# U products of 40 tokens from gathered rows: narrower U chunks, a longer build stage, three row buffers

## The chip, the cores and the metric

The kernel runs on one core of a Trainium2 chip. The metric is the device time of one execution in microseconds. It computes one decoder layer for 512 tokens of width 1024 in float32: a mixer (Mamba-2 heads and latent attention) and then a PEER channel mixer, which chooses among 16384 experts. The change lies in the second part.

## The reference, cut to what matters

```python
def peer(x, w_query, sub_keys, u_table, v_table):      # blocks of 128 tokens
    q = (xb @ w_query).reshape(T, 8, 2, 128)
    s = einsum('thkd,hknd->thkn', q, sub_keys)
    sv, si = top_k(s, 16)                               # each half of each head
    cand_s = sv[:, :, 0, :, None] + sv[:, :, 1, None, :]
    cand_i = si[:, :, 0, :, None] * 128 + si[:, :, 1, None, :]
    top_s, top_pos = top_k(cand_s, 16)
    expert_idx = take_along_axis(cand_i, top_pos)       # 8 x 16 = 128 experts a token
    gate = softmax(top_s)
    act = gelu(einsum('td,thkd->thk', xb, u_table[expert_idx]))
    return einsum('thk,thkd->td', gate * act, v_table[expert_idx])
```

Each token uses 128 of the 16384 experts: the gate times gelu(u_e . x), times the row v_e, summed. Layer norms follow with a residual.

## The kernel before, in words

The 512 tokens are treated in two ways. **Blocks 0 to 2** (384 tokens) are computed densely: for each of 128 *chunks* of 128 experts, TensorE forms u.x for all of the chunk's experts (a *U chunk*, `u_half` at L1295, two halves of 12 matmuls in three-pass float32r), ScalarE applies Gelu into an `act` tile, VectorE multiplies by the gate matrix G (`v_prep`, L1429; G is zero where a token does not use an expert), and TensorE accumulates G.act times v (a *V chunk*, `v_mm`, 18 matmuls of 512 columns). **Block 3** (128 tokens) is computed by gathering: GpSimd fetches the rows u_e and v_e by indirect DMA and VectorE forms dots and sums (`gather`, L1488).

The last UG = 32 tokens of block 2 are a mixture. Their U products come from gathered rows (`ug_fetch`, `ug_dots`, L1128 to L1145): the 32 x 128 pairs of token and expert are laid out as 128 partitions x 32 columns; for column n GpSimd gathers 128 rows of u into a `urow` buffer (UROWS = 4 of them), and VectorE multiplies a row by the token's input `UR["x"]` and sums it, which is one *dot* (L1137). Their products gate x gelu, scaled, then stand in G itself (`ug_head`, L1147, writes them into `gT`), and so U chunks need only NU = 384 - 32 = 352 columns; `v_prep` copies G's last 32 columns as they are (L1437).

The work around the change has this order, all written out by hand, since the kernel records it under a manual schedule:

- The index search for blocks 0 to 2 ends in `decode` (L1033), which yields the expert numbers and gates `IJG[b]`, calls `ug_index` for block 2, two dots, and `g_head(0)`.
- `build_g` (L1187) makes G in 48 *steps* of 8 tokens. `hot(n)` on VectorE writes a one-hot pair (`ij`, L1195) and its product with the gates (`g`, L1202). The product covers a high and a low float16 part; for steps in LOWA, the even ones from 2 to 42, VectorE makes the high part alone (half the size), and ScalarE the low part in 8 copies (L1227), placed behind the evictions of the step before. TensorE multiplies the parts (16 matmuls of 128 columns, L1221 and L1222), ScalarE evicts the result (L1224), and every fourth step G goes to DRAM.
- `g_head(b)` (L1170) transposes the next 16 steps' gates and indices on TensorE; ScalarE copies them, and VectorE subtracts for the low part (L1183).
- `drive` (L1350) fills TensorE with halves of U chunks. It compares two clocks of estimated time, `tm[0]` for TensorE (T_U = 3.9 a U chunk) and `tm[1]` for VectorE, and issues a half when the first is not ahead, or when a minimum (`least`) asks for it. U chunks may run ahead only as far as there is room: LEAD = 56 `act` tiles, of which KEEP = 42 exist from the start, and 14 in the room of the pool `ug` (rows and inputs of the dots), which opens when the dots are done.
- After `build_g` the remaining U chunks up to LEAD follow, then V chunks, alternating with U chunks until these are through, and the gather of block 3 goes on beside them, paced by `GS` and ENDU so that it ends some chunks before the last V chunk. The V items from 121 on (LASTC = 120) use freed tiles and are multiplied block by block at the end, followed by the last layer norms.

Weights come through one stream (`Stream`): SP's queue loads 512 KB into one of three raw buffers (L93), ScalarE makes the rounded high part (L111), VectorE the difference (a *split*, L121), three buffers of each.

Of the kernel before, what the change touches and what calls it, by code (L numbers as in the profile page):

```python
# [11 lines left out]
F32 = mybir.dt.float32  # L12
# [3 lines left out]
I32 = mybir.dt.int32  # L16
U32 = mybir.dt.uint32
AF = mybir.ActivationFunctionType
OP = mybir.AluOpType
# [5 lines left out]
D = 1024  # L25
# [3 lines left out]
NEG = -1.0e30  # L29
SCALE = 192.0 ** -0.5  # L30
NT = 384
UG = 32
NU = NT - UG
LEAD = 56
KEEP = 42
UROWS = 4
RES = 2
LASTC = 120
T_U = 3.9
T_Q = 6.3  # L40
ROWS = 5
ENDU = 12
WV = 0.86
GST = (1, 3, 5, 7)
LOWA = range(2, 44, 2)
# [10 lines left out]
def tile_block(ctx: ExitStack, tc: tile.TileContext, I, out):  # L56
    nc = tc.nc
    ctx.enter_context(tc.manual_schedule())
    V, A, T, G = nc.vector, nc.scalar, nc.tensor, nc.gpsimd
# [158 lines left out]
    xsp = dram.tile([NB, 128, D], F32, name="xsp")  # L218
# [3 lines left out]
    ugi = dram.tile([UG, 128], I32, name="ugi")  # L222
    ugg = dram.tile([UG, 128], F32, name="ugg")
# [375 lines left out]
    for i in range(13):  # L599
        ps = proj(i)  # L600
# [511 lines left out]

    GT, UR = {}, {}

    def ug_index(tmp):
        ijg = IJG[2]
        f = lambda z: z.rearrange("p h k -> p (h k)")
        ix = tmp[:, :128].bitcast(I32)
        V.scalar_tensor_tensor(ix, f(ijg[:, 0]), 128.0, f(ijg[:, 1]), op0=OP.mult, op1=OP.add)
        G.dma_start(ugi, ix[128 - UG:])  # L1120
        G.dma_start(ugg, f(ijg[128 - UG:, 2]))
        G.dma_start(UR["ix"], bass.AP(tensor=ugi.tensor, offset=ugi.offset, ap=[[UG, 128 // UG], [128, UG], [1, UG]]))
        G.dma_start(UR["g"], ugg)
        for n in range(UROWS):
            ug_fetch(n)
        UR["dots"] = ug_dots()

    def ug_fetch(n):  # L1128
        if n < UG:
            UR[n] = ug.tile([128, D], F32, name="urow", bufs=UROWS)  # L1130
            G.indirect_dma_start(out=UR[n], out_offset=None, in_=I["u"],
                                 in_offset=bass.IndirectOffsetOnAxis(ap=UR["ix"][:, n:n + 1], axis=0))

    def ug_dots():
        for n in range(UG):
            r = UR.pop(n)
            V.scalar_tensor_tensor(r, r, 1.0, UR["x"], op0=OP.mult, op1=OP.mult, accum_out=UR["hd"][:, n:n + 1])  # L1137
            ug_fetch(n + UROWS)
            yield 1.2
        A.activation(UR["hd"], UR["hd"], AF.Gelu)  # L1140
        G.dma_start(bass.AP(tensor=ugh.tensor, offset=ugh.offset, ap=[[UG, 128 // UG], [128, UG], [1, UG]]), UR["hd"])
        G.dma_start(UR["w"], ugh)
        close(ug)
        aps.append(pool("act2"))
        yield 0.1  # L1145
# [24 lines left out]
    def g_head(b):  # L1170
        ijg = IJG.pop(b)
        ps = px()
        for x, e in enumerate((0, 1, 0, 2)):
            T.transpose(ps[:, x * 128:(x + 1) * 128], ijg[:, e].rearrange("p h k -> p (h k)"), ident)
        ijT = ijp.tile([128, 8, 2, 2, 8], F16, name="ijT", bufs=2)
        gT = ijp.tile([128, 16, 2, 8], F16, name="gT", bufs=2)
        gL = ijp.tile([128, 16, 8], F32, name="gL", bufs=2)
        gv = ps[:, 384:512].rearrange("p (n t) -> p n t", t=8)
        for r in range(2):
            src = bass.AP(tensor=ps.tensor, offset=ps.offset + r * 136, ap=[ps.ap[0], [128, 2], [16, 8], [1, 8]])  # L1180
            A.activation(ijT[:, :, r].rearrange("p n e t -> p e n t"), src, AF.Copy)
        A.activation(gT[:, :, 0], gv, AF.Copy, scale=GSC)
        V.scalar_tensor_tensor(gT[:, :, 1], gv, GSC, gT[:, :, 0], op0=OP.mult, op1=OP.subtract)  # L1183
        A.activation(gL, gT[:, :, 1], AF.Copy)
        GT[b] = ijT, gT, gL

    def build_g():  # L1187
        jij = gb.tile([128, 4, 4, 128, 2], F16, name="ij")

        def hot(n):  # L1190
            ijT, gT, gL = GT[n // 16]
            r = n % 2
            col = ijT[:, n % 16 // 2, r].rearrange("p e (q c) -> p (e q) c", c=2)
            b2 = [128, 8, 128, 2]
            V.tensor_tensor(jij[:, 2 * r:2 * r + 2].rearrange("p e q i c -> p (e q) i c"), iotaE[:, None].to_broadcast(b2),  # L1195
                            col[:, :, None, :].to_broadcast(b2), op=OP.is_equal)
            oj, oi = jij[:, 1 + r], jij[:, 3 * r]
            g = gb.tile([128, 2, 4, 128, 2], F16, name="g", bufs=2)
            ne = 1 if n in LOWA else 2
            b4 = [128, ne, 4, 128, 2]  # L1200
            gv = gT[:, n % 16, :ne].rearrange("p e (q c) -> p e q c", c=2)
            V.tensor_tensor(g[:, :ne], oi[:, None].to_broadcast(b4), gv[:, :, :, None, :].to_broadcast(b4), op=OP.mult)  # L1202
            low = [(g[:, 1, t // 2, :, t % 2], oi[:, t // 2, :, t % 2], gL[:, n % 16, t:t + 1]) for t in range(8)]
            return oj, g[:, 0], g[:, 1], low if ne == 1 else []

        nxt = hot(0)
        dots, head = UR["dots"], ug_head()
        tm[1] += 3.0
        yield 2.6
        for n in range(48):  # L1210
            b, g = divmod(n, 16)
            oj, oi, g1, _ = nxt
            if n < 47:
                nxt = hot(n + 1)
            if g % 4 == 0:
                stg = gs[n // 4 % 2].tile([128, 128, 32], F32, name="stg")
            for hf in range(2):
                ps = pw()
                for t in range(4):
                    q, c = hf * 2 + t // 2, t % 2  # L1220
                    T.matmul(ps[:, t * 128:(t + 1) * 128], oj[:, q, :, c], oi[:, q, :, c], start=True, stop=False)  # L1221
                    T.matmul(ps[:, t * 128:(t + 1) * 128], oj[:, q, :, c], g1[:, q, :, c], start=False, stop=True)  # L1222
                q0 = g % 4 * 8 + hf * 4
                A.activation(stg[:, :, q0:q0 + 4],  # L1224
                             ps.rearrange("p (t i) -> p i t", t=4), AF.Copy, scale=1.0 / GSC)
            for o, i, z in nxt[3] if n < 47 else ():
                A.activation(o, i, AF.Copy, scale=z)  # L1227
            tm[0] += 0.95
            if n == 32:
                least[0] = 0  # L1230
            if g % 4 == 3:
                nc.scalar.dma_start(gs0[b * 4 + g // 4], stg[:, 0:8])
                nc.scalar.dma_start(gsp[b * 4 + g // 4], stg[:, 8:])
            if g == 12 and b < 2:
                g_head(b + 1)
            for _ in range(2 if n % 3 == 2 and n < 18 else 1):
                tm[1] += next(dots, 0.0)
            if n in range(36, 41):
                tm[1] += next(head)
            yield (1.9 if n + 1 in LOWA else 2.42) if n < 47 else 0.1  # L1240

    bal = [0.0]
# [45 lines left out]
    def act_tile():  # L1288
        k = an[0] % LEAD >= KEEP
        an[0] += 1  # L1290
        return aps[k].tile([128, NU], F32, name="act", bufs=LEAD - KEEP if k else KEEP)

    UO = {}

    def u_half(c, e, psum=None):  # L1295
        if e == 0:
            UO[c] = [z.rearrange("p (k j) -> p k j", k=8) for z in item()] + [(psum or pu)()[:, :NU]]
        h, l, ps = UO[c]
        for k in range(4 * e, 4 * e + 4):
            mm3(ps, h[:, k], l[:, k], XTH[:, k, :NU], XTL[:, k, :NU], k == 0, k == 7)  # L1300
        if e:
            del UO[c]
            ACT[c] = act_tile()
            A.activation(ACT[c], ps, AF.Gelu)  # L1304

    def u_chunk(c, psum=None):
        for e in range(2):
# [32 lines left out]
    def step_u():  # L1340
        e = len(UO)
        u_half(un[0], e)
        un[0] += e
        tm[0] += T_U / 2
        if not e and lo_on[0] is V:
            tm[1] += 1.2

# [16 lines left out]
    for m in range(17):  # L1364
# [9 lines left out]
        while tm[1] < tm[0] + T_Q:  # L1374
            c = next(fill, None)
            if c is None:
# [3 lines left out]
    drive(fill)  # L1380
    close(rq)
    ug = pool("ug")
    UR["x"] = ug.tile([128, D], F32, name="ux")
    nc.sync.dma_start(UR["x"], bass.AP(tensor=xsp.tensor, offset=xsp.offset + (3 * 128 - UG) * D,
                                       ap=[[0, 128 // UG], [D, UG], [1, D]]))
    UR["ix"] = ijp.tile([128, UG], I32, name="uix")
    UR["hd"] = ijp.tile([128, UG], F32, name="uhd")
    UR["g"] = ijp.tile([UG, 128], F32, name="ugw")
    rt2 = pool("rt2")
# [39 lines left out]
    def v_prep(c):  # L1429
        load_g(c // 4)  # L1430
        if c % 4 == 0:
            load_g(c // 4 + 1)
        a = ACT.pop(c)
        P = vst.tile([128, NT], F32, name="P", bufs=2)
        V.tensor_tensor(P[:, :NU].rearrange("p (b t) -> p b t", t=32), a.rearrange("p (b t) -> p b t", t=32),
                        gt[c // 4][:, :NU // 32, c % 4, :], op=OP.mult)
        A.activation(P[:, NU:], gt[c // 4][:, NU // 32, c % 4, :], AF.Copy)  # L1437
        if c % 4 == 3:
            gt.pop(c // 4)
        return P  # L1440
# [284 lines left out]
```

## Time and profile before

| | |
|---|---|
| time, median of 3 runs | 1601.49 us (1599.5 to 1602.77) |
| profiled execution | 1602.0 us, span 1600.2 us |
| TensorE busy | 1576.7 us, 99% of the span |
| VectorE busy | 1343.8 us, 84% |
| ScalarE busy | 754.5 us, 47% |
| GpSimd busy | 554.6 us, 35% |
| HBM read, written | 368.40 MB, 31.80 MB |
| dots of the 32 tokens (L1137) | 32, 568.5 to 696.8 us from the start |
| first V matmul | 794.53 us |

A row of a group of instructions reads: line, engine, operation, out<-in, sizes, count, then busy time and mean duration in ns, then the idle time of the engine before them with what ended it. A row in order of time reads: start in us, duration in us, engine, line, operation. PE is TensorE, PEld its weight loads, DVE VectorE, ACT ScalarE, POOL GpSimd, SP the engine that issues most DMAs. Durations of neighbours overlap slightly, so the cost of one in a row of many is read from start to start.

### The profile page before, as it was taken

Reading aid. Unit: us, or ns where it says so; the run is one execution under the profiler, and the core shown is the slowest. Engines: PE = TensorE matmul, PEld = TensorE weight load, DVE = VectorE, ACT = ScalarE, POOL = GpSimd, SP = SyncE. Lnnn points to the kernel's source line nnn. Section 1 sums busy time; section 2 is a strip of 40 time slices with the busy share of each in tenths; the row PEclk is TensorE's granted clock in tenths of the full one; section 3 lists DMA queues with packets and bytes.
Section 4 is the critical chain, followed back from the end, with each engine's and each line's share of the span. In section 5 each row is a group of like instructions: output and inputs, shape, how many; then the busy total and the mean of one; then the engine's idle time right before and its main releaser. Section 6 shows DMA issues by size and latency. Waiting matters only on the chain.

```text
span 1600.2 us, 24088 instructions
## 1 busy us (share of the span) xinstructions
PE 1576.7 (99%) x8699; PEld 1386.3 (87%) x8699; DVE 1343.8 (84%) x2545; ACT 754.5 (47%) x1409; POOL 554.6 (35%) x400
## 2 busy tenths in 40 slices
PE   9999999999999999999999999999999999999997
PEld 7887888888888999988899999999999999888886
DVE  8978677647799999988579888888888988998987
ACT  5564467731433457778553333334333433443442
POOL 0000032600244144400026546565555555654410
PEclk9999999999999999999999999999999999999999
DMA  6242122473332479965779999999999999999973
GB/s 249 97 154 93 47 78 59 140 246 126 123 97 88 142 240 371 352 255 196 270 242 365 373 350 358 334 379 358 336 354 365 357 344 358 371 353 334 343 256 141
DMA packets 154555, 403.88 MB, mean 252 GB/s; under 512 B 13036, under 2 KB 65964, under 8 KB 152644
## 3 DMA queue, kind: packets, MB, share of 16 engines
q1 hardware_dynamic: 104948, 213.19, 39.4%
q0 software_dynamic: 45888, 163.73, 27.6%
q10 hardware_dynamic: 3600, 25.43, 4.1%
q8 instruction: 68, 1.11, 0.3%
q14 instruction: 51, 0.42, 0.1%
HBM read 368.40 MB, written 31.80 MB: 250 GB/s over the span
## 4 chain that ended last, share of the span: by engine, by line
PE 83%; DVE 12%; ACT 3%; DMA 1%; issue 1%; DVEq 0%; ACTq 0%
PE va L1473 10%; PE va L1472 10%; PE va L1476 10%; PE pu L74 10%; PE pu L75 10%; PE pu L76 10%; PE pa L75 3%; PE pa L76 3%; PE pa L74 3%; PE pw L75 1%; PE pw L1222 1%; PE pw L76 1%; PE pw L74 1%; DVE t L1004 1%; PE pw L1221 1%
## 5 line engine op out<-in xcount | busy, mean ns | idle before, releaser
L111 ACT ACTIVATE wih<-wir 128x1024 fp32r<-128x1024 f32 (+2 forms) x269 | 277.8, 1033 | 310.4 <-DMA wir<-v 107.4
L121 DVE TENSOR_TENSOR wil<-wir,wih 128x1024 fp32r<-128x1024 f32 (+1 forms) x235 | 284.2, 1210 | 102.6 <-ACT wih L111 46.0
L76 PE MATMUL pu<-XTH,wil 128*128 128x352 f32 x1008 | 325.8, 323 | 0.0
L74 PE MATMUL pu<-XTH,wih 128*128 128x352 f32 x896 | 293.9, 328 | 0.4 <-ACT act L1304 0.4
L75 PE MATMUL pu<-XTL,wih 128*128 128x352 f32 x896 | 290.2, 324 | 0.0
L1473 PE MATMUL va<-wil,Ph 128*128 128x512 f32 x726 | 282.9, 390 | 0.0
L1510 POOL DMA_INDIRECT row<-u,ix x128 | 192.0, 1500 | 219.0 <-DVE row L1521 115.9
L1510 POOL DMA_INDIRECT row<-v,ix x128 | 188.8, 1475 | 174.8 <-DVE ac L1527 149.2
L76 PEld LDWEIGHTS pu<-XTH,wil 128*128 128x128 f32 x1008 | 190.7, 189 | 0.0
L74 PEld LDWEIGHTS pu<-XTH,wih 128*128 128x128 f32 x896 | 169.7, 189 | 4.7 <-ACT act L1304 0.7
L75 PEld LDWEIGHTS pu<-XTL,wih 128*128 128x128 f32 x896 | 170.0, 190 | 2.8
L1472 PE MATMUL va<-wih,Ph 128*128 128x512 f32 x438 | 170.7, 390 | 0.0
L1527 DVE SCALAR_TENSOR_TENSOR ac<-row,hd,ac 128x1024 f32<-128x1024 f32 x128 | 164.0, 1281 | 2.9 <-DMA row<-v,ix 0.8
L1473 PEld LDWEIGHTS va<-wil,Ph 128*128 128x128 f32 x726 | 136.3, 188 | 25.9
L1521 DVE SCALAR_TENSOR_TENSOR row<-row,x 128x1024 f32<-128x1024 f32 x128 | 150.5, 1221 | 4.2 <-DMA row<-u,ix 4.1
L1476 PE MATMUL va<-wih,Pl 128*128 128x512 f32 x438 | 134.9, 389 | 0.0
L111 ACT ACTIVATE wihx<-wir 128x1024 fp32r<-128x1024 f32 x67 | 71.0, 1060 | 126.8 <-DMA wir<-v 95.1
L1304 ACT ACTIVATE act<-pu 128x352 f32<-128x352 f32 x126 | 58.0, 460 | 141.6 <-PE pu L76 138.8
L121 POOL TENSOR_TENSOR wil<-wir,wih 128x1024 fp32r<-128x1024 f32 (+3 forms) x34 | 70.5, 2081 | 154.7 <-PE pw L76 100.2
L1472 PE MATMUL va<-wihx,Ph 128*128 128x512 f32 x288 | 112.3, 390 | 0.0
L121 DVE TENSOR_TENSOR wil<-wir,wihx 128x1024 fp32r<-128x1024 f32 x62 | 75.8, 1222 | 32.0 <-issue 17.2
L1476 PEld LDWEIGHTS va<-wih,Pl 128*128 128x128 f32 x438 | 82.2, 188 | 17.3
(500 smaller groups left out, 3238.0 us busy)
## 6 DMA issues: line engine op xcount, KB each, us to landing
wir<-ut SPq DMA_DIRECT2D x128, 512.0 KB
wir<-v SPq DMA_DIRECT2D x128, 512.0 KB
gsp<-stg ACTq DMA_DIRECT2D x12, 1920.0 KB
gt<-gsp SPq DMA_DIRECT2D x30, 768.0 KB
wir<-wo SPq DMA_DIRECT2D x26, 512.0 KB
wir<-wf SPq DMA_DIRECT2D x18, 512.0 KB
wir<-wqr SPq DMA_DIRECT2D x16, 512.0 KB
de<-acd POOLq DMA_DIRECT2D x8, 512.0 KB
```

What stands on the lines that cost most here:

```text
L74: T.matmul(ps, lh, rh, start=start, stop=False)
L75: T.matmul(ps, lh, rl, start=False, stop=False)
L76: T.matmul(ps, ll, rh, start=False, stop=stop)
L111: A.activation(h, r, AF.Copy)
L121: self.lo(n).tensor_tensor(l, r, h, op=OP.subtract)
L1304: A.activation(ACT[c], ps, AF.Gelu)
L1472: T.matmul(va[b][e], Ph[b], h[:, cs], start=c == 0, stop=False)
L1473: T.matmul(va[b][e], Ph[b], l[:, cs], start=False, stop=False)
L1476: T.matmul(va[b][e], Pl[b], h[:, cs], start=False, stop=c == 127)
L1510: G.indirect_dma_start(out=R[s], out_offset=None, in_=I["u"] if s < 128 else I["v"], in_offset=bass.IndirectOffsetOnAxis(ap=ix[:, s % 128: ...
L1521: V.scalar_tensor_tensor(r, r, 1.0, x3, op0=OP.mult, op1=OP.mult, accum_out=hd[:, s:s + 1])
L1527: V.scalar_tensor_tensor(ac, r, hd[:, s - 128:s - 127], ac, op0=OP.mult, op1=OP.add)
```

## The change

The mixture takes 40 tokens instead of 32, and U chunks 344 columns instead of 352. The 40 tokens are two sets of 32 and 8 (UGS), each laid out over 128 partitions, with index tiles of their own; the second set's inputs `ux` are loaded by SP's queue into the same buffer after dot 31, and the two calls that follow do no dot. There are 40 dots, placed as two in the steps n = 2, 6, 10, 14, 18, 22, 28, 30 and one in the others, so that they end in step 31 instead of 23, and three row buffers instead of four. The `act` tiles keep a pitch of 352 columns; KEEP is 45, and 11 open after the dots. Until then `drive` counts a U chunk at 4.25, afterwards at 3.8 (T_U). The 8 low copies of a step come ahead of the matmuls and evictions of the step before, the subtraction for the low part three steps after its transposes (`g_low`), and `ug_head` is called in three steps instead of five. `v_prep` multiplies 320 + 24 columns and copies 8 + 32. ENDU is 11.

```diff
-UG = 32
+UG = 40
+UGS = ((32, 8), (8, 0))
 NU = NT - UG
 LEAD = 56
-KEEP = 42
-UROWS = 4
+KEEP = 45
+AW = 352
+UROWS = 3
-T_U = 3.9
+T_U = 3.8
-ENDU = 12
+ENDU = 11
...
+    def ug_x(j, c, o):
+        UR["x", j] = ug.tile([128, D], F32, name="ux")
+        nc.sync.dma_start(UR["x", j], bass.AP(tensor=xsp.tensor, offset=xsp.offset + (3 * 128 - UG + o) * D,
+                                              ap=[[0, 128 // c], [D, c], [1, D]]))
...
         for n in range(UG):
+            if n == UGS[0][0]:
+                ug_x(1, *UGS[1])
+                yield 0.0
+                yield 0.0
             r = UR.pop(n)
-            V.scalar_tensor_tensor(r, r, 1.0, UR["x"], op0=OP.mult, op1=OP.mult, accum_out=UR["hd"][:, n:n + 1])
+            V.scalar_tensor_tensor(r, r, 1.0, UR["x", int(n >= UGS[0][0])], op0=OP.mult, op1=OP.mult, accum_out=UR["hd"][:, n:n + 1])
             ug_fetch(n + UROWS)
             yield 1.2
         A.activation(UR["hd"], UR["hd"], AF.Gelu)
-        G.dma_start(bass.AP(tensor=ugh.tensor, offset=ugh.offset, ap=[[UG, 128 // UG], [128, UG], [1, UG]]), UR["hd"])
+        for j, (c, o) in enumerate(UGS):
+            n0 = j * UGS[0][0]
+            G.dma_start(ug_ap(ugh, c, o), UR["hd"][:, n0:n0 + c])
...
+        GT[b] = ijT, gT, gL
+        GT["lo"] = gv, gT, gL
+
+    def g_low():
+        gv, gT, gL = GT.pop("lo")
         V.scalar_tensor_tensor(gT[:, :, 1], gv, GSC, gT[:, :, 0], op0=OP.mult, op1=OP.subtract)
         A.activation(gL, gT[:, :, 1], AF.Copy)
-        GT[b] = ijT, gT, gL
...
-            low = [(g[:, 1, t // 2, :, t % 2], oi[:, t // 2, :, t % 2], gL[:, n % 16, t:t + 1]) for t in range(8)]
-            return oj, g[:, 0], g[:, 1], low if ne == 1 else []
+            for t in range(8 if ne == 1 else 0):
+                A.activation(g[:, 1, t // 2, :, t % 2], oi[:, t // 2, :, t % 2], AF.Copy, scale=gL[:, n % 16, t:t + 1])
+            return oj, g[:, 0], g[:, 1]
...
-            for o, i, z in nxt[3] if n < 47 else ():
-                A.activation(o, i, AF.Copy, scale=z)
...
-            if g == 12 and b < 2:
+            if g == 11 and b < 2:
                 g_head(b + 1)
-            for _ in range(2 if n % 3 == 2 and n < 18 else 1):
+            if g == 14 and b < 2:
+                g_low()
+            for _ in range(2 if n % 4 == 2 and n < 24 or n in (28, 30) else 1):
                 tm[1] += next(dots, 0.0)
-            if n in range(36, 41):
-                tm[1] += next(head)
+            if n in (36, 37, 38):
+                tm[1] += next(head) + next(head, 0.0)
...
-        tm[0] += T_U / 2
+        tm[0] += (T_U if len(aps) > 1 else 4.25) / 2
...
-        V.tensor_tensor(P[:, :NU].rearrange("p (b t) -> p b t", t=32), a.rearrange("p (b t) -> p b t", t=32),
-                        gt[c // 4][:, :NU // 32, c % 4, :], op=OP.mult)
-        A.activation(P[:, NU:], gt[c // 4][:, NU // 32, c % 4, :], AF.Copy)
+        g, nb, rm = gt[c // 4][:, :, c % 4], NU // 32, NU % 32
+        N0, N1 = nb * 32, (nb + 1) * 32
+        V.tensor_tensor(P[:, :N0].rearrange("p (b t) -> p b t", t=32), a[:, :N0].rearrange("p (b t) -> p b t", t=32),
+                        g[:, :nb], op=OP.mult)
+        V.tensor_tensor(P[:, N0:NU], a[:, N0:NU], g[:, nb, :rm], op=OP.mult)
+        A.activation(P[:, NU:N1], g[:, nb, rm:], AF.Copy)
+        A.activation(P[:, N1:], g[:, nb + 1], AF.Copy)
```

More of the change, by code (lines that the diff above doesn't have):

```diff
@@ L1113, in tile_block @@
     GT, UR = {}, {}
+    ug_ap = lambda t, c, o: bass.AP(tensor=t.tensor, offset=t.offset + o * 128, ap=[[c, 128 // c], [128, c], [1, c]])
+    def ug_x(j, c, o):
+        UR["x", j] = ug.tile([128, D], F32, name="ux")
+        nc.sync.dma_start(UR["x", j], bass.AP(tensor=xsp.tensor, offset=xsp.offset + (3 * 128 - UG + o) * D,
+                                              ap=[[0, 128 // c], [D, c], [1, D]]))
     def ug_index(tmp):
@@ L1121, in ug_index @@
         G.dma_start(ugg, f(ijg[128 - UG:, 2]))
-        G.dma_start(UR["ix"], bass.AP(tensor=ugi.tensor, offset=ugi.offset, ap=[[UG, 128 // UG], [128, UG], [1, UG]]))
-        G.dma_start(UR["g"], ugg)
+        for j, (c, o) in enumerate(UGS):
+            G.dma_start(UR["ix"][j], ug_ap(ugi, c, o))
         for n in range(UROWS):
             ug_fetch(n)
+        G.dma_start(UR["g"], ugg)
         UR["dots"] = ug_dots()
@@ L1129, in ug_fetch @@
         if n < UG:
+            c0 = UGS[0][0]
+            j, m = (0, n) if n < c0 else (1, n - c0)
             UR[n] = ug.tile([128, D], F32, name="urow", bufs=UROWS)
             G.indirect_dma_start(out=UR[n], out_offset=None, in_=I["u"],
-                                 in_offset=bass.IndirectOffsetOnAxis(ap=UR["ix"][:, n:n + 1], axis=0))
+                                 in_offset=bass.IndirectOffsetOnAxis(ap=UR["ix"][j][:, m:m + 1], axis=0))
     def ug_dots():
         for n in range(UG):
+            if n == UGS[0][0]:
+                ug_x(1, *UGS[1])
+                yield 0.0
+                yield 0.0
             r = UR.pop(n)
-            V.scalar_tensor_tensor(r, r, 1.0, UR["x"], op0=OP.mult, op1=OP.mult, accum_out=UR["hd"][:, n:n + 1])
+            V.scalar_tensor_tensor(r, r, 1.0, UR["x", int(n >= UGS[0][0])], op0=OP.mult, op1=OP.mult, accum_out=UR["hd"][:, n:n + 1])
             ug_fetch(n + UROWS)
@@ L1140, in ug_dots @@
         A.activation(UR["hd"], UR["hd"], AF.Gelu)
-        G.dma_start(bass.AP(tensor=ugh.tensor, offset=ugh.offset, ap=[[UG, 128 // UG], [128, UG], [1, UG]]), UR["hd"])
+        for j, (c, o) in enumerate(UGS):
+            n0 = j * UGS[0][0]
+            G.dma_start(ug_ap(ugh, c, o), UR["hd"][:, n0:n0 + c])
         G.dma_start(UR["w"], ugh)
@@ L1211, in build_g @@
             b, g = divmod(n, 16)
-            oj, oi, g1, _ = nxt
+            oj, oi, g1 = nxt
             if n < 47:
@@ L1233, in build_g @@
                 nc.scalar.dma_start(gsp[b * 4 + g // 4], stg[:, 8:])
-            if g == 12 and b < 2:
+            if g == 11 and b < 2:
                 g_head(b + 1)
-            for _ in range(2 if n % 3 == 2 and n < 18 else 1):
+            if g == 14 and b < 2:
+                g_low()
+            for _ in range(2 if n % 4 == 2 and n < 24 or n in (28, 30) else 1):
                 tm[1] += next(dots, 0.0)
-            if n in range(36, 41):
-                tm[1] += next(head)
+            if n in (36, 37, 38):
+                tm[1] += next(head) + next(head, 0.0)
             yield (1.9 if n + 1 in LOWA else 2.42) if n < 47 else 0.1
@@ L1290, in act_tile @@
         an[0] += 1
-        return aps[k].tile([128, NU], F32, name="act", bufs=LEAD - KEEP if k else KEEP)
+        return aps[k].tile([128, AW], F32, name="act", bufs=LEAD - KEEP if k else KEEP)
     UO = {}
@@ L1303, in u_half @@
             ACT[c] = act_tile()
-            A.activation(ACT[c], ps, AF.Gelu)
+            A.activation(ACT[c][:, :NU], ps, AF.Gelu)
     def u_chunk(c, psum=None):
@@ L1382, in tile_block @@
     ug = pool("ug")
[L1383 to L1386, printed above, removed]
+    ug_x(0, *UGS[0])
+    UR["ix"] = [ijp.tile([128, c], I32, name=f"uix{c}") for c, _ in UGS]
     UR["hd"] = ijp.tile([128, UG], F32, name="uhd")
```

## The prediction

> **What bounds the kernel now.** I read the page first (engines, then the chain), then the span by stages, then the order of time in the stage that the change rewrites.
>
> ```profile
> span 1600.2 us, 24088 instructions
> PE 1576.7 (99%) x8699; PEld 1386.3 (87%) x8699; DVE 1343.8 (84%) x2545; ACT 754.5 (47%) x1409; POOL 554.6 (35%) x400
> ```
>
> TensorE is busy 99% of the span, but busy counts overlapping matmuls, so the stages decide:
>
> ```profile
> 545.00:690.00 145.00, 144.84 (x1117) 141.18 (x1118) 140.00 (x159) 96.20 (x205) 57.11 (x36) 1.00 0.84 306
> 690.00:780.00 90.00, 82.56 (x713) 75.32 (x713) 73.11 (x76) 69.20 (x167) 1.84 (x3) 0.95 0.62 219
> 800.00:1140.00 340.00, 340.00 (x1801) 309.20 (x1800) 286.43 (x430) 133.50 (x219) 179.59 (x120) 1.00 0.95 346
> 1140.00:1520.00 380.00, 380.00 (x1874) 332.78 (x1873) 338.40 (x377) 148.94 (x261) 198.24 (x136) 1.00 0.97 351
> ```
>
> The columns are length, then busy time of PE, PEld, DVE, ACT, POOL, the granted clock, DMA share and GB/s. Three regimes. From 545 to 690 us (gate matrices G, the dots of the gathered rows, U chunks as filler) TensorE is full and VectorE nearly so (140.00 of 145). From 690 to 780 us both have holes: TensorE 82.56 of 90, VectorE 73.11. From 800 us on (V chunks, with U chunks up to about 1360 us) TensorE alone is full.
>
> **Term 1, U chunks behind the build stage.** Each is 24 matmuls of 352 columns, beside V chunks of 18 matmuls of 512:
>
> ```profile
> 897.68 0.39 PE L1472 MATMUL va<-wihx,Ph 128*128 128x512 f32 x1
> 901.78 0.33 PE L74 MATMUL pu<-XTH,wih 128*128 128x352 f32 x1
> 905.62 0.39 PE L1472 MATMUL va<-wih,Ph 128*128 128x512 f32 x1
> ```
>
> A V chunk takes 901.78 - 897.68 = 4.10 us, 0.228 a matmul; a U chunk 3.84, 0.160 a matmul. So 160 columns cost 0.068 us, 0.42 ns each, and eight fewer save 3.4 ns a matmul, 0.081 us a chunk. In the built order 71 U chunks stand behind the first V matmul: 71 x 0.081 = 5.8 us, on the path, since TensorE is full there. VectorE and ScalarE get two small operations per V chunk more (24 columns of product, 8 columns of copy). Nearest rows:
>
> ```profile
> 760.34 0.19 DVE L1166 SCALAR_TENSOR_TENSOR gT<-px,gT 128x32 f16<-128x32 f32 x1 [0.33 <-ACT gT L1164]
> L1437 ACT ACTIVATE P<-gt 128x32 f32<-128x32 f32 x128 | 27.9, 218 | 1.5 <-DMA gt<-gs 1.5
> ```
>
> At 0.19 and 0.22 us that is 24 and 28 us over 128 chunks, beside TensorE: VectorE has 338.40 of 380 us in use, and 0.19 per 4.1 us chunk brings its 89% to about 94%. It costs nothing except in the tail (term 4), where that cover is gone.
>
> By contrast the Trainium skill, page "TensorE: Matmul & The Clock Gate", section "Back-to-back issue gap", gives sustained spacings of about 81 ns at 128 columns and 131 ns at 512. By that slope, 0.13 ns a column, my estimate is that eight columns save 1.0 ns and the 71 chunks 1.8 us; the two spacings above disagree with it (0.42 ns), and I go by them.
>
> **Term 2, VectorE from build step 0 to the last dot.** The steps are laid end to end on VectorE:
>
> ```profile
> 583.18 1.22 DVE L121 TENSOR_TENSOR wil<-wir,wih 128x1024 fp32r<-128x1024 f32 x1
> 584.31 1.22 DVE L1195 TENSOR_TENSOR ij<-iotaE,ijT 128x2048 f16<-128x2048 f16 x1
> 585.57 1.23 DVE L1202 TENSOR_TENSOR g<-ij,gT 128x2048 f16<-128x2048 f16 x1
> 586.71 1.22 DVE L1137 SCALAR_TENSOR_TENSOR urow<-urow,ux 128x1024 f32<-128x1024 f32 x1
> 587.85 0.09 DVE L1137 DVE_READ_ACCUMULATOR urow<-urow,ux 128x1 f32 x1
> 587.85 1.23 DVE L121 TENSOR_TENSOR wil<-wir,wih 128x1024 fp32r<-128x1024 f32 x1
> 588.99 1.22 DVE L1195 TENSOR_TENSOR ij<-iotaE,ijT 128x2048 f16<-128x2048 f16 x1
> 590.25 0.69 DVE L1202 TENSOR_TENSOR g<-ij,gT 128x1024 f16<-128x1024 f16 x1
> 590.86 1.22 DVE L1137 SCALAR_TENSOR_TENSOR urow<-urow,ux 128x1024 f32<-128x1024 f32 x1
> ```
>
> From start to start: split S (L121) 1.14, one-hot I (L1195) 1.26, full H (L1202, 2048) 1.14, half H 0.61, dot D 1.14. Before, the built order has 25 I, 13 full and 12 half H, 30 D and 23 S up to the last dot: 31.5 + 14.8 + 7.3 + 34.2 + 26.2 = 114.0. The trace takes it from 580.78 to 696.8:
>
> ```profile
> 579.44 0.29 DVE L1183 SCALAR_TENSOR_TENSOR gT<-px,gT 128x128 f16<-128x128 f32 x1 [2.40 <-ACT gT L1182]
> 580.78 1.22 DVE L1195 TENSOR_TENSOR ij<-iotaE,ijT 128x2048 f16<-128x2048 f16 x1
> 695.62 1.22 DVE L1137 SCALAR_TENSOR_TENSOR urow<-urow,ux 128x1024 f32<-128x1024 f32 x1
> 778.08 1.23 DVE L1202 TENSOR_TENSOR g<-ij,gT 128x2048 f16<-128x2048 f16 x1
> ```
>
> that is 116.0: VectorE sets this stretch, with 2 us of waits. After, the dots reach to step 31 and the count is 33 I, 17 full and 16 half H, 38 D, 28 S: 41.6 + 19.4 + 9.8 + 43.3 + 31.9 = 146.0, or 32.0 more. Two splits fewer stand before step 0 (-2.3), and the 2.40 wait at L1183 should go, since the low part now comes some operations after its copy (-2.4; 0 if ScalarE is late again).
>
> New is the wait for rows: three buffers instead of four. In the new order about 22 of the 40 dots have only two steps between a dot's end and the dot three later: 2 x 1.26 + 1.14 + 0.61 + two dots 2.3 + two splits 2.3 = 8.8 us (7.7 to 9.0); the rest have 11 to 12 (before: 13 or more). A fetch is POOL's issue and a 512 KB load, bounded by two such loads in the chain of waits:
>
> ```profile
> L1131 POOL DMA_INDIRECT urow<-u,uix x32 | 54.8, 1713 | 71.2 <-DVE urow L1137 65.4 <-issue 5.8
> 534.97 6.39 DMA wir<-ut
> 1562.67 8.38 DMA wir<-v
> ```
>
> 1.7 + 6.4 = 8.1 us fits (wait 0); 1.7 + 8.4 = 10.1 does not: 1.3 us a dot, and if it comes back at 14 or 15 of the 22, 19 us. I take 4, nearer the short load, since DMA is 0.84 busy there and not 0.95. The eight added fetches cost POOL 14 us, which has 57 of 145 in use. The second set's row of inputs is loaded by SP's queue after dot 31: queued behind it are U's weight loads, which wait for later VectorE splits anyway, and dot 32 comes two steps (some 9 us) on, so 0, at most 2. The last dot then ends at 696.8 + 32.0 - 4.7 + 4 = 728.1 (724 to 743).
>
> **Term 3, the rest of the build stage.** Before, 696.8 to the last H (778.08 + 1.14 = 779.2) is 82.4 us for 23 steps, 3.58 each, with holes on both engines. ScalarE explains them:
>
> ```profile
> L1227 ACT ACTIVATE g<-ij,gL 128x128 f16<-128x128 f16 x168 | 52.2, 435 | 0.5 <-DVE ij L1195 0.4
> L1224 ACT ACTIVATE stg<-pw 128x512 f32<-128x512 f32 x96 | 51.6, 595 | 7.3 <-PE pw L1222 7.0
> PE pw L1221 <- DVE g L1202: 4.1, 3, 1.7
> PE pw L1221 <- ACT g L1227: 1.9, 1, 1.9
> ```
>
> Eight low copies (8 x 0.31 = 2.5 us) wait in ScalarE's queue behind two evictions (2 x 0.54) of the step before, and that step's matmuls before those. The change puts the copies ahead of the evictions. Afterwards 15 steps are left, with 8 splits: VectorE alone needs 15 x 1.26 + 10 x 1.14 + 5 x 0.61 + 8 x 1.14 + about 2 for U's scaling = 44.4; at the old rate they take 15 x 3.58 = 53.7. I take 48, as one of two causes of holes goes. The last H ends at 776.1, not 779.2. Behind it stand 3.5 U chunks before the first V matmul instead of 3:
>
> ```profile
> 794.53 0.40 PE L1472 MATMUL va<-wih,Ph 128*128 128x512 f32 x1
> ```
>
> 15.3 us becomes 15.3 + 0.5 x 3.76 - 3 x 0.08 = 16.9. V starts at 793.0: terms 2 and 3 together give -1.5, with ends at 724 + 44.4 + 16.9 = 785.3 (-9) and 743 + 53.7 + 16.9 = 813.6 (+19).
>
> **Term 4, the tail.** ENDU 11 and the new pace put the gather's final normalisation one V chunk later, between the splits of V items 120 and 121. These rows are the end of the chain:
>
> ```profile
> 1545.26 1.22 DVE L121 TENSOR_TENSOR wil<-wir,wihx 128x1024 fp32r<-128x1024 f32 x1 [0.82 <-PE va L1473]
> 1546.40 1.28 DVE L187 BATCH_NORM_STATS2 lgst<-ac 128x6 f32<-128x512 f32 x2
> 1549.76 0.56 DVE L1463 TENSOR_TENSOR Pl<-P,Ph 128x384 fp32r<-128x384 f32 x1
> 1561.43 1.22 DVE L121 TENSOR_TENSOR XTL<-wir,XTL 128x1024 fp32r<-128x1024 f32 x1
> 1571.13 1.07 ACT wihx L111
> 1572.22 1.24 DVE wil L121
> ```
>
> The split at 1561.43 (item 124) frees a raw buffer, the last load (8.38 above) follows, its split ends at 1573.5, and TensorE takes it up at once. Before, the normalisation (1546.40 to 1549.76, 3.36) stands behind item 119's split, and 11.7 us of chunks and gather work follow until item 124's. After, item 120's split starts a V chunk later, at 1545.26 + 4.08 = 1549.3; then 1.14 + 3.36 and the 11.7, less one split and one product and difference (1.14 + 0.9), plus four small products of 0.15: item 124 comes at 1564.1, 2.6 us late. With an 8.4 us load TensorE waits 2.6, with a 6 us one nothing. I take +2.
>
> **Sum.** -1.5 - 5.8 + 2 = -5.3. The profiled execution took 1602.0 us (span 1600.2), 0.5 above the median of 1601.49; so 1596.7, or 1596 against the median. About 0.2% (3.2 us) is what can be told from no change.
>
> **Rivals.** *Rows (slower).* VectorE waits at the dots for the third buffer: 19 us instead of 4, all ahead of G, and -5.3 becomes +9.7: 1611 us. It decides once the wait exceeds some 12 us, about 0.55 us at each of the 22 dots. For: VectorE sets that stretch, and U work cannot fill it (45 chunks of room). Against: each wait lengthens the next gaps. 0.27.
>
> *The build stage gains more.* No row wait and VectorE end to end after the dots: -4 - 3.6 further, 1588 us. For: ScalarE's order; against: both engines then have under 10% left. 0.15.
>
> *Columns save nothing.* 344 is no multiple of 32, and all widths in the trace are; were 344 to run like 352, the 5.8 would go and the time be about 1602. Against: 352 and 512 lie on one slope, but nothing shows a width between. The skill's spacing rule above would give 1600. 0.08.
>
> **Numbers.** The forecast has 0.50: 0.47 of it faster by over 0.2%, 0.03 within. Rows: 0.26 slower, 0.01 within. The larger gain is faster, the column case within. Faster 0.62, within 0.12, slower 0.26. The range from 1587 to 1609 takes in the bounds of terms 2 to 4 but the far ends of the row wait and of the gain; without the rivals it would be 1590 to 1602.
>
> **What would show it.** U matmuls at 0.157 us from start to start; first V matmul near 793; no 2.4 us gap on VectorE before the first low part of G; gaps before the dots with the gathered row as releaser, 4 us in sum; last split about 2 us later against TensorE's last chunk. A first V matmul behind 797, or row waits over 12 us, makes the prediction wrong.

## The result, and the profile after

The changed kernel takes 1614.3 us (median of 6 runs, 1611.1 to 1619.0) where the kernel before takes 1601.8 us (6 runs beside it): 1.0082 times as long, 95% interval 1.0058 to 1.0105. It is slower; 1596 us, faster, was forecast. The profiled execution took 1611.5 us. The six times lie in two groups, 1611.1 to 1611.5 and 1617.1 to 1619.0; the profile is one of the first group, and what makes the second is not shown.

Page and stages of the changed kernel, in the columns used for the kernel before:

```profile
span 1609.7 us, 24388 instructions
PE 1575.4 (98%) x8699; PEld 1376.1 (85%) x8699; DVE 1358.7 (84%) x2689; ACT 764.8 (48%) x1537; POOL 564.6 (35%) x410
```

```profile
545.00:690.00 145.00, 136.35 (x1033) 126.51 (x1033) 135.19 (x155) 90.09 (x202) 54.18 (x37) 0.99 0.81 284
690.00:742.00 52.00, 44.68 (x340) 41.75 (x339) 40.61 (x48) 31.14 (x75) 13.04 (x8) 0.90 0.77 282
742.00:792.00 50.00, 49.70 (x433) 45.91 (x432) 44.75 (x48) 40.46 (x95) 2.44 (x4) 0.97 0.73 255
820.00:1140.00 320.00, 319.70 (x1710) 289.51 (x1710) 276.67 (x450) 131.68 (x251) 176.09 (x116) 1.00 0.96 350
```

From 545 to 690 us TensorE was full before (144.84 of 145) and is not now (136.35); VectorE has 135.19 instead of 140.00. From 690 to 742 us both are worse, and the granted clock is 0.90. After the dots, from 742 us on, the build stage is denser than it was.

Who waits on VectorE up to the last dot (us in total, times, longest), and the same by its group of instructions:

```profile
DVE urow L1153 <- DMA urow<-u,uix: 14.7, 7, 4.2
DVE urow L1153 <- DMA ux<-xsp: 5.0, 1, 5.0
DVE ij L1217 <- PE pw L1246: 1.6, 1, 1.6
```

```profile
L1153 DVE SCALAR_TENSOR_TENSOR urow<-urow,ux 128x1024 f32<-128x1024 f32 x38 | 46.2, 1220 | 19.7 <-DMA urow<-u,uix 14.7 <-DMA ux<-xsp 5.0
```

So 19.7 us of waits stand before the dots: 14.7 for gathered rows, 5.0 for the second set's inputs (`ux`). In the profile of before there were none:

```profile
L1137 DVE SCALAR_TENSOR_TENSOR urow<-urow,ux 128x1024 f32<-128x1024 f32 x32 | 38.6, 1219 | 0.0
```

The row waits are seven. Five of them, 12.8 us, come about 20 us apart, at 611, 632, 652, 673 and 695 us: one in each round of four steps, as often as the store of G's bulk. The longest of the row waits, in order of time, first on VectorE, then on POOL:

```profile
682.19 1.22 DVE L1153 SCALAR_TENSOR_TENSOR urow<-urow,ux 128x1024 f32<-128x1024 f32 x1
686.33 1.22 DVE L1153 SCALAR_TENSOR_TENSOR urow<-urow,ux 128x1024 f32<-128x1024 f32 x1
689.88 1.22 DVE L1153 SCALAR_TENSOR_TENSOR urow<-urow,ux 128x1024 f32<-128x1024 f32 x1
695.27 1.22 DVE L1153 SCALAR_TENSOR_TENSOR urow<-urow,ux 128x1024 f32<-128x1024 f32 x1 [4.17 <-DMA urow<-u,uix]
...
683.69 1.69 POOL L1143 DMA_INDIRECT urow<-u,uix  x1 [2.99 <-DVE urow L1153]
```

The dot of 682.19 frees a buffer, POOL issues the fetch from 683.69 to 685.38, and the dot three later, the second of a double, can start only at 695.27: 11.6 us after the issue began, 9.9 after it ended. What the queues moved meanwhile, from 686 to 690 us and then from 692 to 696 us (packets, MB, share of 16 engines; q10 carries ScalarE's stores, q0 POOL's transfers, q1 SyncE's):

```profile
q10 hardware_dynamic: 95, 1.43, 84.1%
q1 hardware_dynamic: 34, 0.14, 8.5%
q0 software_dynamic: 12, 0.05, 2.8%
...
q0 software_dynamic: 334, 1.18, 73.8%
q1 hardware_dynamic: 32, 0.07, 4.2%
q10 hardware_dynamic: 2, 0.02, 0.9%
```

For four microseconds the 1920 KB store of G's bulk (`gsp`, every fourth step) has the DMA engines nearly to itself, and most of the rows come after that.

### The profile page after: what moved, and what is told of

Its sections match the earlier page's. It is cut to its first block, busy times and chain, and to the rows that moved or that the text cites. A ratio compares the mean times of both kernels' runs of the same rounds, so it can differ in the third digit from the quotient of the medians.

```text
span 1609.7 us, 24388 instructions
## 1 busy us (share of the span) xinstructions
PE 1575.4 (98%) x8699; PEld 1376.1 (85%) x8699; DVE 1358.7 (84%) x2689; ACT 764.8 (48%) x1537; POOL 564.6 (35%) x410
## 4 chain that ended last, share of the span: by engine, by line
PE 71%; DVE 13%; issue 8%; POOL 3%; DMA 3%; ACT 2%; DVEq 0%; SPq 0%; POOLq 0%; ACTq 0%
PE va L1498 10%; PE va L1499 10%; PE va L1502 10%; PE pu L76 7%; PE pu L78 7%; PE pu L77 7%; POOL urow L1143 3%; PE pa L78 3%; PE pa L77 3%; PE pa L76 3%; PE pw L77 1%; PE pw L78 1%; PE pw L76 1%; DVE t L1006 1%; DVE wil L123 1%
## 5 line engine op out<-in xcount | busy, mean ns | idle before, releaser
L78 PE MATMUL pu<-XTH,wil 128*128 128x344 f32 x1008 | 322.9, 320 | 3.0 <-DVE wil L123 3.0
L76 PE MATMUL pu<-XTH,wih 128*128 128x344 f32 x896 | 289.5, 323 | 0.0
L77 PE MATMUL pu<-XTL,wih 128*128 128x344 f32 x896 | 286.5, 320 | 0.0
L1143 POOL DMA_INDIRECT urow<-u,uix x40 | 64.2, 1606 | 111.3 <-DVE urow L1153 107.1
L1498 PEld LDWEIGHTS va<-wih,Ph 128*128 128x128 f32 x438 | 82.2, 188 | 17.8 <-ACT Ph L1481 1.7
```

The costliest lines, as they stand in the source:

```text
L76: T.matmul(ps, lh, rh, start=start, stop=False)
L77: T.matmul(ps, lh, rl, start=False, stop=False)
L78: T.matmul(ps, ll, rh, start=False, stop=stop)
L1498: T.matmul(va[b][e], Ph[b], h[:, cs], start=c == 0, stop=False)
```

## The experiments

Times are medians; the ratios are to the kernel before on the same chip, whose median was 1601.2 to 1603.1 us in the three sets of runs. Waits and starts are those of the one profiled execution of each run.

**Three rows alone.** The kernel before, with one edit:

```
-UROWS = 4
+UROWS = 3
```

> The kernel before with three row buffers instead of four and nothing else. Theory (rows): a dot and the one three later then leave 8.8 us, and fetches that are issued beside a store of G land after 8.5 to 9.5 us, so waits of 4 to 12 us come before dots, and the time rises by 3 to 10 us (1605 to 1612). Rivals (thinner U work; more dots): no change, 1601 to 1603 us.

Measured 1612.5 us, ratio 1.0045 (1.0022 to 1.0069). Its profiled execution took 1611.3 us, with 12.2 us of waits at the dots, the last dot at 706.0 instead of 696.8 and V at 804.3 instead of 794.5:

```profile
L1137 DVE SCALAR_TENSOR_TENSOR urow<-urow,ux 128x1024 f32<-128x1024 f32 x30 | 36.3, 1218 | 12.2 <-DMA urow<-u,uix 12.2
```

The waits and the time are just above the ranges of the theory (4 to 12 us, 1605 to 1612 us), and the rivals' "no change" is out. Of the 12.2 us of waits, 9.3 reach the end (1602.0 to 1611.3).

**Four rows again in the changed kernel.** They fit only with three places fewer for U activations:

```
-KEEP = 45
-UROWS = 3
+KEEP = 42
+UROWS = 4
```

> The changed kernel with four row buffers again; the fourth takes the room of three act tiles, so KEEP is 42 and 14 tiles open after the dots. Theory (rows): the waits before the dots for a gathered row, 14.7 us in the changed kernel, fall to under 2 us, the 5.0 us wait for the second set's inputs stays; VectorE reaches the end of the dots near 726 instead of 742 us, and the time falls by 10 to 14 us to 1598 to 1602 us. Rival (thinner U work): TensorE's idle time comes from counting a U chunk at 4.25, so four rows change little: over 1608 us. Rival (more dots on VectorE): the added operations are the price, rows or not: over 1608 us.

Measured 1617.7 us, ratio 1.0082 (1.0059 to 1.0104): a miss. The waits did fall, to 10.6 us (5.7 for rows, where under 2 were expected, and 4.8 for `ux`), and the last dot came at 730.2, 12 us earlier; but V started at 810.5, 3 us later. The stage cut at the 42nd and 43rd U activation shows why:

```profile
575.60:716.00 140.40, 131.06 (x1075) 122.39 (x1073) 130.67 (x154) 98.74 (x230) 55.77 (x34) 0.98 0.88 314
716.00:737.00 21.00, 11.65 (x76) 10.33 (x77) 15.41 (x21) 10.87 (x29) 3.85 (x4) 0.67 0.65 255
737.00:810.50 73.50, 69.86 (x575) 66.72 (x573) 48.15 (x50) 46.36 (x103) 1.09 (x2) 0.98 0.68 228
```

The 42nd activation is written at 716 us, no 43rd until the dots' room comes free, and for 21 us TensorE has 11.65 us of work and a clock of 0.67. From the last dot to V it is then 80.3 us instead of 65.3: the U chunks missed are made up there. It suggested a second price, room, and a run for it:

**The room alone.** The kernel before with

```
-KEEP = 42
+KEEP = 39
```

> The kernel before with room for 39 U activations instead of 42 until the first products are done; nothing else differs. Theory A (that room sets how much TensorE has to do while VectorE builds, and the loss of three places is what ate the 12 us that the fourth row gave in the run with 42 places): the last dot stays at 695 to 699 us, the first matmul of V moves from 794.5 to 800 or later, and the time is 1608 to 1614 us. Rival B (three places cost nothing by themselves): 1600 to 1605 us.

Measured 1611.7 us, ratio 1.0058 (1.0038 to 1.0078). The last dot comes even earlier, at 693.0, and V starts at 803.8, 9.3 us later: theory A. The stage up to the 39th U activation, to the 40th, and to V:

```profile
580.50:677.00 96.50, 96.44 (x791) 93.29 (x790) 94.38 (x113) 70.73 (x156) 40.03 (x24) 1.00 0.89 331
677.00:700.00 23.00, 16.17 (x125) 13.71 (x123) 19.89 (x24) 15.47 (x41) 4.15 (x3) 0.70 0.74 273
700.00:803.80 103.80, 97.83 (x777) 91.03 (x776) 68.12 (x69) 68.61 (x158) 1.05 (x2) 0.95 0.60 208
```

Three places are worth 9 us to V's start, about 3 us each. So in this stage two things are on the path at once: VectorE's dots, and enough room for U chunks to occupy TensorE until the last of them.

**Without the thinner U work.** The changed kernel with

```
-        tm[0] += (T_U if len(aps) > 1 else 4.25) / 2
+        tm[0] += T_U / 2
```

> The changed kernel with each U chunk counted at 3.8 us from the start, instead of 4.25 us until the room of the first products is free. Theory A (the thinner U work is harmless, it only spreads 45 places over the longer stretch): the dot waits stay near 20 us, and the time is 1608 to 1615 us; if the places run out early, TensorE idles before the last dot and it is up to 1620 us. Rival B (the thinner work leaves TensorE idle and its clock low during the dots, and that is part of the loss): 1602 to 1607 us.

Measured 1636.3 us, ratio 1.0218 (1.0191 to 1.0246), worse than either theory; theory A had the places run out, but only to 1620 us. The 45th activation is written at 715 us and the 46th at 750:

```profile
579.40:715.00 135.60, 130.13 (x1044) 123.38 (x1043) 120.69 (x141) 91.39 (x203) 47.16 (x30) 0.98 0.84 303
715.00:750.00 35.00, 21.45 (x152) 18.25 (x150) 26.71 (x35) 20.82 (x58) 9.04 (x7) 0.54 0.72 267
```

The thinner work is no part of the loss; it saves some 22 us (ratio 1.0082 against 1.0218) by making 45 places last to 739 us.

**The store in four parts.** The changed kernel, each part issued one step after the other:

```
+        old = None
...
-                nc.scalar.dma_start(gsp[b * 4 + g // 4], stg[:, 8:])
+                old = gsp[b * 4 + g // 4], stg
+            if old:
+                for k in range(4) if n == 47 else (g % 4 - 3 & 3,):
+                    nc.scalar.dma_start(old[0][:, k * 30:k * 30 + 30], old[1][:, 8 + k * 30:38 + k * 30])
```

> The changed kernel, with each 2 MB store of G's bulk cut into four 0.5 MB parts issued one build step apart; nothing else differs. Theory A (row fetches and the second inputs' load stand behind the whole store, which three rows cannot cover): the waits for rows fall from 14.7 us to 6 or less, the wait for ux from 5.0 us to 2 or less, the last dot ends 9 to 15 us earlier (727 to 733 us) and the time is 1598 to 1605 us. Rival B (three rows are too few whatever the store does): the waits stay at 12 to 17 us for rows and the time at 1609 to 1614 us.

Measured 1607.4 us, ratio 1.0039 (1.0021 to 1.0058); profiled 1602.8 us, V at 799.7. Between the theories:

```profile
L1153 DVE SCALAR_TENSOR_TENSOR urow<-urow,ux 128x1024 f32<-128x1024 f32 x38 | 46.2, 1219 | 11.5 <-DMA urow<-u,uix 9.5 <-DMA ux<-xsp 1.9
```

The `ux` wait falls to 1.9 us as expected, the row waits only from 14.7 to 9.5. Storing in one piece is behind 8 of the 20 us, and between the two profiles they came back in full (1611.5 to 1602.8); this profile is the fastest of its ten runs, and by the ratios it is 7 us (1.0082 to 1.0039). The remainder stays with the store spread. From the start of POOL's issue, which takes up to 1.7 us of it, a fetch lands after 7.4 us (median), which the 8.8 us between dots cover:

```profile
urow<-u,uix POOLq DMA_INDIRECT x40, 7.4
```

But the spread is wide: the five fetches that cost a dot over 0.3 us took 9.3 to 11.0 us, where the dots left 7.7 to 9.1.

**The doubles one step later**, in the changed kernel, then with the store in parts, then with the second set's inputs loaded early into a tile of their own, which takes three U places:

```
-            for _ in range(2 if n % 4 == 2 and n < 24 or n in (28, 30) else 1):
+            for _ in range(2 if n % 4 == 3 and n < 24 or n in (28, 30) else 1):
```

> The changed kernel with the first six double dots one step later (n = 3, 7, 11, 15, 19, 23 instead of 2, 6, ... 22), still three rows. The distances between a dot and the one three later are the same (7.7 to 12.4 us), but the row that is fetched beside a store of G is then needed three steps later. Theory (the store of G holds a fetch up, and the double dot behind it waits): row waits under 5 us instead of 14.7, 1600 to 1605 us. Rival (three rows are too few wherever the doubles stand): waits as before, 1609 to 1615 us.

> The changed kernel with the store of G's bulk in four parts one step apart, and the doubles of the first 24 steps one step later. Theory A (with the store spread, what is left is the short time that a double leaves for the third row, and that does not depend on where the double stands): waits of 9 to 13 us, 1604 to 1609 us. Rival B (a double right after the first part still meets the most of the store, and moving it helps further): waits of 8 us or less, 1599 to 1604 us.

> The changed kernel with the doubles of the first 24 steps one step later, and with the second set's inputs in a tile of their own that is loaded at the start, which takes three of the 45 places for U activations. Theory A (waits are what counts, room is not): waits for rows 8 to 11 us, none for ux, the last dot at 730 to 735 us, time 1600 to 1605 us. Rival B (room counts as much as the waits): the last dot comes as early, but V does not start before 806 us and the time is 1609 to 1618 us.

The shift alone: 1609.5 us (1.0038, 1.0015 to 1.0061). The row waits fell to 9.6 us, between the two theories, but the `ux` wait grew to 7.1; the time is at the lower end of the rival's range. With the parts: 1607.1 us (1.0026, 1.0008 to 1.0043), waits of 7.5 for rows and 4.5 for `ux`. The time is theory A's; that the shift adds nothing to the parts fits it, but the row waits alone would be theory B's. With early inputs and 42 places: 1613.2 us (1.0076, 1.0044 to 1.0107). The `ux` wait is gone and the last dot comes at 731.7, as theory A had it, helped by the two calls without a dot, which this run leaves out. But V starts at 805.1: the time is theory B's (V a little before its 806), and the row waits, 13.5 us, did not fall to 8 to 11 either.

The profiles of the first two runs are slow ones among their own (1614.7 and 1617.3 us). In both, TensorE stops once between 1360 and 1380 us, for 3.3 and 3.8 us, waiting for ScalarE's `Ph` of a V chunk, long after the dots:

```profile
PE va L1498 <- ACT Ph L1481: 3.3, 1, 3.3
PE va L1502 <- ACT Ph L1485: 3.8, 1, 3.8
```

So not all that varies between runs lies in the build stage. What makes this stop, and whether it makes the slower group of the changed kernel's runs, is not shown.

**No waits at all.** The changed kernel in the same order and room and with as many fetches, but no dot depends on a transfer:

```
-            UR[n] = ug.tile([128, D], F32, name="urow", bufs=UROWS)
-            G.indirect_dma_start(out=UR[n], ...
+            if "one" not in UR:
+                UR["one"] = ug.tile([128, D], F32, name="urow1")
+            UR[n] = UR["one"]
+            dump = ug.tile([128, D], F32, name="urow", bufs=UROWS - 1)
+            G.indirect_dma_start(out=dump, ...
...
-                ug_x(1, *UGS[1])
+                UR["x", 1] = UR["x", 0]
...
-            V.scalar_tensor_tensor(r, r, 1.0, UR["x", int(n >= UGS[0][0])], ...
+            V.scalar_tensor_tensor(r, UR["x", 0], 1.0, UR["x", int(n >= UGS[0][0])], ...
```

> The changed kernel in the same order of instructions, but no dot waits for a transfer: the rows still arrive, into two tiles that nothing reads, every dot multiplies the first set's inputs by themselves into the third tile, and the second set's inputs are not loaded. The row products are left out of the result by this. Theory A (the 19.7 us of waits are the whole difference from the forecast): the last dot at 720 to 724 us, and the time is 1611.5 - 19.7 = 1592, so 1589 to 1596 us. Rival B (the waits lay beside TensorE work that is needed anyway, so that only part of them returns): 1597 to 1604 us.

Measured 1592.7 us, ratio 0.9945 (0.9925 to 0.9966); profiled 1590.6 us, 20.9 less than the changed kernel, whose waits were 19.7. Before the dots 0.3 us are left:

```profile
L1156 DVE SCALAR_TENSOR_TENSOR urow<-ux 128x1024 f32<-128x1024 f32 x38 | 46.4, 1220 | 0.3
```

Up to the last dot, and from there to V, first in this run, then in the changed kernel:

```profile
575.40:723.30 147.90, 143.02 (x1189) 134.60 (x1189) 146.02 (x174) 108.81 (x254) 54.36 (x34) 0.99 0.90 323
723.30:787.50 64.20, 63.38 (x537) 59.24 (x536) 47.90 (x53) 46.12 (x106) 2.44 (x4) 1.00 0.82 282
```

```profile
575.40:742.20 166.80, 152.63 (x1201) 140.05 (x1200) 145.94 (x174) 108.63 (x254) 56.63 (x36) 0.97 0.83 297
742.20:807.50 65.30, 64.61 (x537) 60.54 (x536) 47.90 (x53) 46.22 (x106) 2.44 (x4) 0.97 0.78 263
```

VectorE does the same 146 us of work in 147.9 or in 166.8 us, 18.9 of the 20.9. From the last dot to V it is 1.1 us, and from V to the end 0.9. Theory A. Two things differ beside the waits: the fetches are paced by the two tiles that nothing reads and no longer by the dots, and the 512 KB of the second set's inputs are not loaded.

**What beats both.** The kernel before (32 tokens, four rows, 42 places) with two parts of the change alone: the low copies issued with the one-hots, ahead of the evictions, and the low part of G's scaling three steps after its copy:

```
...
+            for t in range(8 if ne == 1 else 0):
+                A.activation(g[:, 1, t // 2, :, t % 2], oi[:, t // 2, :, t % 2], AF.Copy, scale=gL[:, n % 16, t:t + 1])
...
-            if g == 12 and b < 2:
+            if g == 11 and b < 2:
                 g_head(b + 1)
+            if g == 14 and b < 2:
+                g_low()
```

> The kernel before with the two moves of the low part alone: the eight copies ahead of the evictions of the step before, the subtraction three steps after its transposes; 32 tokens, four rows, dots and U work as before. If the ScalarE order held build steps up, the stretch from the last dot to the last build step takes 72 to 78 us instead of 82.4, VectorE's 2.4 us waits at the subtraction go, and the time falls by 4 to 10 us (1592 to 1598). If the rate of that stretch comes from U work alone, it stays within 2 us of 1601.8.

> The kernel before (32 tokens, four rows) with the low copies ahead of the evictions and the low parts three steps later, as in the run that measured 1598.9 us, and in addition the store of G's bulk in four parts one step apart. Theory A (four rows hide the store, so cutting it does nothing): 1597 to 1600.5 us. Rival B (the whole store also holds up the weights' loads behind TensorE's work after the dots): 1593 to 1596.5 us.

The first measured 1598.9 us, ratio 0.9968 (0.9950 to 0.9985), V at 790.6 instead of 794.5. The fall of 4 to 5 us is in the range that was expected (the time just above its 1598), and the waits at the subtraction are gone; but the stretch from the last dot to the last build step takes 79.7 us, not 72 to 78. So ScalarE's order held that stretch up by less than 3 us of 82.4. With the store in parts besides, 1598.7 us, ratio 0.9972 (0.9962 to 0.9981): theory A, four rows hide the store, and cutting it adds nothing.

## Why the prediction was wrong

By its own steps, in the profiled executions:

- **Term 1 held.** U matmuls go from 159.9 to 156.1 ns start to start (means over the 1,704 and 1,703 spacings behind V's start, one stop left out): 6.5 us where 5.8 was forecast. The slope of the Trainium skill's page "TensorE: Matmul & The Clock Gate", section "Back-to-back issue gap", gave 1.8 us; the trace does not agree. The width of 344, no multiple of 32, costs nothing extra here, so *columns save nothing* fell too. Its premise was misread: the profile of before has 64 matmuls of 384 columns, which lie between 352 and 512, and 20 of 16 columns or one.
- **Term 4 did not show, and the V stage held in sum by luck.** From V's start to the end: 805.7 before, 802.2 after, -3.5, where -5.8 + 2 = -3.8 was forecast. But from the last U matmul to the end it is 243.2 us instead of 242.6, not 2 us more, and TensorE does not stop for the last load. In its place the V matmuls are about 1 ns further apart over all 2,303 spacings, 2 to 3 us, which no term had; why is not shown.
- **Term 3's number held, its reason only in part.** The last build step ends 48.8 us after the last dot and V starts 16.4 us later, forecast 48 and 16.9. But the 48 was put down to ScalarE's order, and the run with that order alone went from 3.58 to 3.46 us a step (79.7 us for 23 steps): 1.8 us over 15 steps, of the 4.9 that the stage gained on the old rate (53.7). What brought the rest stays open.
- **Term 2 held but for its waits.** VectorE's work from step 0 to the last dot is 145.94 us, forecast 146.0; step 0 starts at 575.4, forecast 576.1, and the 2.40 us gap at the low part is gone:

```profile
574.09 1.22 DVE L123 TENSOR_TENSOR wil<-wir,wih 128x1024 fp32r<-128x1024 f32 x1
575.23 0.28 DVE L1206 SCALAR_TENSOR_TENSOR gT<-px,gT 128x128 f16<-128x128 f32 x1
575.42 1.22 DVE L1217 TENSOR_TENSOR ij<-iotaE,ijT 128x2048 f16<-128x2048 f16 x1
```

The step that failed is term 2's wait for rows. "I take 4, nearer the short load, since DMA is 0.84 busy there and not 0.95": it measured 14.7; and "0, at most 2" for the second set's inputs measured 5.0. With 19.7 for 4 the sum is -5.3 + 15.7 = +10.4; measured +9.5 (1602.0 to 1611.5). The medians differ by 12.5 (1601.8 to 1614.3); the 3 us more come from the second group of runs, of which there is no profile. That is the rival *Rows*, and its 1611 us is the time of the profile. But its 19 us agree partly by luck: it had 14 or 15 waits of 1.3 us for rows alone, and there were seven, five of them 1.6 to 4.2 us, and one of 5.0 for `ux`. Without waits the sum says -9.3, and the run without waits gave -10.2 (1602.9 to 1592.7).

Why I took 4: I read the DMA share as an average over 145 us and chose the load time from it. In that stretch every fourth step holds a burst of a 2 MB store, and a fetch beside it is late: the longest wait followed one that took 11.6 us with its issue. So the upper bound of 10.1 us was too low as well, since it came from a load of a stretch without such a store. In the profile of before these fetches made no dot wait, because four rows left 13 us and more for one; but their lateness was there to be read, and the expectation of the run with three rows alone has it (8.5 to 9.5 us). Not all of the wait is the store: with it in parts, 11.5 of the 19.7 us remained.

What I had not priced at all is the room. Here the change kept it (45 places, thinner work), so no term is wrong for it; but the run that gives back the fourth row shows that row buffers and U places cannot both be had: the fourth row alone cost 7 to 10 us (ratio 1.0045; V 9.7 us later), three places some 9 (ratio 1.0058; V 9.3 us later).

## What to carry to other kernels

A buffer count is judged against the slowest transfer in the stage, not the stage's mean DMA share: look for large stores that recur on another queue, and put the worst fetch beside the shortest gap between uses. Where two uses share one pool of memory, price a place of each before trading them: here the fourth row was worth 7 to 10 us, and three places of filler work about as much. To learn what a set of waits costs, keep the instructions and cut the dependence: one run (1592.7 us) separated the one bad term, 19.7 us, from the rest of the sum.

## What was not expected of the hardware

A store of 1920 KB on ScalarE's queue moved 1.43 MB in four microseconds while the row queue, with a fetch issued, moved 0.05 MB. The Trainium skill's page "DMA: Bandwidth & Descriptors", section "Queues, rings and completion order", says that each engine takes turns between the queues it has work for, packet by packet. In these four microseconds, 95 packets to 12, the trace does not show even turns, but in the next one, from 690 to 691 us, it nearly does:

```profile
q10 hardware_dynamic: 18, 0.15, 36.3%
q1 hardware_dynamic: 32, 0.13, 31.8%
q0 software_dynamic: 29, 0.12, 28.8%
```

So the fetch lost its time before its packets began to move, about 4 us after POOL's issue had ended; the fetch issued at 696.77 us, with no store beside it, took about 2. What holds the start back, and whether the queue had packets to offer until then, is not shown.

TensorE's clock fell without one long stop. In the run without thinner work it was granted 0.54 over 35 us in which TensorE was busy 21.45 us, and from 713 to 742 us it was at half:

```profile
713.00:742.00 29.00, 15.04 (x116) 12.09 (x116) 23.46 (x30) 16.44 (x45) 7.69 (x5) 0.50 0.79 287
```

No single wait of a G matmul in the whole stage was longer than 4.7 us, and that one ended at 742.6 us; until then none was longer than 2.6 us:

```profile
PE pw L1245 <- DVE g L1224: 17.7, 14, 4.7
```

In this run, thinly spread work was paid for twice, in idle time and in clock.
